# Row tiles in five buffers and earlier accumulator additions in the second output projection of a decoder layer

## The chip, the cores and the metric

The kernel runs on one core of a Trainium2 chip. The metric is device time in microseconds (us) of one execution. An execution was also recorded by the hardware profiler; everything that is said of engines, waits and loads comes from that record. The engines are TensorE (PE in the profile, with its weight loads as PEld), VectorE (DVE), ScalarE (ACT), GpSimd (POOL) and SyncE (SP), which here issues most of the transfers (DMAs) between the chip's main memory and its on-chip memory. Each engine works through its own queue strictly in the order of the program; engines wait for each other by semaphores.

## The reference

The reference is one layer of a decoder trunk, in float32, on 1024 positions of 1024 channels. The part around the change:

```python
mix = (jax.nn.sigmoid(gate_a) * y_a + jax.nn.sigmoid(gate_b) * y_b) @ w_o[l]
h = layer_norm(DN_ALPHA * h + mix, ln1_g[l], ln1_b[l])
ffn = conv_ffn(h, w_ffn_up[l], ffn_dw_w[l], ffn_dw_b[l], w_ffn_down[l])
h = layer_norm(DN_ALPHA * h + ffn, ln2_g[l], ln2_b[l])
```

So the product with `w_o` (the output projection) is added to the scaled residual `h`, normalised over the 1024 channels of each position, and the result is what the up projection of the FFN reads.

## The kernel before

The positions are worked in two halves of 512. The first half's normalised rows have long been stored in main memory (`h1_scr`) when the part of this document begins; the second half's output projection is the function `out_proj_pairs`. All products are made in three matmuls each (lines 175, 176 and 177): weights and data are split into a high and a low part, and the product of the two low parts is left out. ScalarE makes the high part (a cast, L141 for weights) and VectorE the low part (a subtraction, L142).

**Rows.** A row tile `r` holds 128 positions by 1024 channels, 4 KB on each partition. `ffn_blocks` makes eight of them under one tag with three buffers: r0 to r3 (`rows`) are the first half's rows, loaded back from `h1_scr` at L927, and r4 to r7 (`rest`) take the second half's residual `h`, loaded at L875. With three buffers, r3 takes the buffer that r0 leaves, r4 that of r1, and so on.

**The first half's rows** are transposed on TensorE (L935, four 128x128 transposes to a bank of PSUM, two banks a row tile), and split into `h1b1` by ScalarE (L940) and VectorE (L941); a plain copy is kept in `h1raw` (L950).

**The second half** is projected in two pairs of row tiles. For each pair there are four PSUM accumulators (tag `acc`, four banks in all), and eight weight tiles `w_wo` are loaded, split and multiplied. Then VectorE adds each accumulator to its half of a row tile (L894), which frees the bank, and `ln_stats` and `ln_apply` normalise the row tiles (statistics at L220 and L234, the root on ScalarE at L235, then L236, L240 and L243). For each finished row tile `block_sums` runs: it stores the row, transposes it, and forms the sums that a Strassen-like scheme for the up projection needs (tiles `ts0`, `ts1` and `ts2`; the results go to `h1s1` to `h1s3` and `h1b2`). GpSimd does the additions L965 and L971 for the first three tiles, VectorE for the fourth.

**What follows.** `up_first` computes, for the first eight column tiles of the FFN's up projection, two products that need only the first half's `h1b1`, so they can run while the second half is being normalised. Its weights are `w_ue0` to `w_ue6` (tag `w` of a pool with three buffers, so that `w_ue3` takes the buffer that `w_ue0` leaves). For each column tile one PSUM bank collects the product with block `b11` (12 matmuls); ScalarE copies it out (`first0_j`, L1015); then the product with block `b21` (12 more) is added on top in the same bank, and copied out again (`first1_j`). The tiles `first` have two buffers and are stored to main memory by DMAs from ScalarE's queue (L1016).

**Memory.** The on-chip memory is given out from two ends. `ffn_blocks` works in a pool `trans` that grows from the left and ends with the function; the pool `firsts` of `up_first` is opened after that at the right, below the block sums' results. In the built program of the kernel before, `trans` ends at byte 169472 of a partition, the last two tiles in it being the two buffers of `ts2`, and `firsts` begins at byte 175872. Where a later tile covers bytes of a tile of an earlier pool, its first writer waits for the last user of the earlier one.

**What sets the order.** A scheduler places the instructions of ScalarE, VectorE, TensorE, GpSimd and SyncE one by one: among those that are ready by its own reckoning the one with the highest priority goes first, priority falling in the order of the code. `tc.high_priority(offset=n)` moves a block ahead by n; the weights' loads and splits have 4000. The order so found is fixed in the program.

Of the kernel before, what the change touches and what calls it, by code (L numbers as in the profile page):

```python
# [8 lines left out]
F32 = mybir.dt.float32  # L9
F32R = mybir.dt.float32r  # L10
AF = mybir.ActivationFunctionType
ALU = mybir.AluOpType
# [4 lines left out]
P = 128  # L17
D = 1024
T = 1024
HALF = 512  # L20
# [8 lines left out]
ALPHA = 2.0 ** 0.25  # L29
# [25 lines left out]
def kernel(  # L55
# [15 lines left out]
    V, A, G, TE, SY = nc.vector, nc.scalar, nc.gpsimd, nc.tensor, nc.sync  # L71
# [14 lines left out]
    def bank(which):  # L86
        n_ps[0] += 1
        pl, tag = (pacc, "acc") if which else (psm, "sm")
        return pl.tile([P, 512], F32, tag=tag, name=f"{tag}{n_ps[0]}")
# [46 lines left out]
    def weights(src, name, pl=None, eng=None, bufs=None):  # L136
        with tc.high_priority(offset=4000):
            st = wst.tile([P, D], F32, tag="st", name=f"st_{name}")
            SY.dma_start(st, src)
            w = (pl or wsp).tile([P, 2, D], F32R, tag="w", bufs=bufs, name=f"w_{name}")  # L140
            A.copy(w[:, 0, :], st)  # L141
            (eng or V).tensor_tensor(  # L142
                out=w[:, 1, :], in0=st, in1=w[:, 0, :].bitcast(F32), op=ALU.subtract
            )
        return w
# [23 lines left out]
    def big_tile(name):  # L169
        return big.tile([P, 2, KD, HALF], F32R, tag="big", name=name)  # L170

    def mm3(ps, wa, xa, start, stop, more=False):


        TE.matmul(ps, wa(0), xa(0), start=start, stop=False, skip_group_check=more)  # L175
        TE.matmul(ps, wa(0), xa(1), start=False, stop=False, skip_group_check=more)  # L176
        return TE.matmul(ps, wa(1), xa(0), start=False, stop=stop, skip_group_check=more)  # L177
# [36 lines left out]
    def row(pl, start, n, name, tag=None):  # L214
        r = pl.tile([P, n], F32, tag=tag or name, name=name)
        SY.dma_start(r, prow[start : start + n].partition_broadcast(P))
        return r
# [4 lines left out]
    def ln_stats(pl, tiles, name, sts=None):  # L222

        n = len(tiles)
        mv = pl.tile([P, n, 2], F32, tag="ln_mv", bufs=2, name=f"mv_{name}")
        rs = pl.tile([P, n], F32, tag="ln_rs", bufs=2, name=f"rs_{name}")
        for i, t in enumerate(tiles):
            if sts:
                st = sts[i]
            else:  # L230
                st = pl.tile([P, 2, 6], F32, tag="ln_st", bufs=2, name=f"st_{name}{i}")
                for q in range(2):
                    ln_part(pl, t, st, q)
            V.bn_aggr(out=mv[:, i, :], in_=st)  # L234
        A.activation(out=rs, in_=mv[:, :, 1], func=AF.Sqrt, bias=eps)  # L235
        V.reciprocal(out=rs, in_=rs)  # L236
        return mv, rs

    def ln_apply(t, mv, rs, i, g, b, op=ALU.subtract):
        V.scalar_tensor_tensor(  # L240
            out=t, in0=t, scalar=mv[:, i, 0:1], in1=g, op0=op, op1=ALU.mult
        )
        V.scalar_tensor_tensor(  # L243
            out=t, in0=t, scalar=rs[:, i : i + 1], in1=b, op0=ALU.mult, op1=ALU.add
        )
# [626 lines left out]
    def out_proj_pairs(pl, rs, mixT, g, b, done):  # L872

        for t in range(4):
            SY.dma_start(rs[t], h_scr[1][t * P : (t + 1) * P, :])  # L875
        for pair in range(2):
            ts = (2 * pair, 2 * pair + 1)
            pss = {(t, q): bank(1) for t in ts for q in range(2)}
            for kp in range(4):
                for q in range(2):  # L880
                    w = weights(wo[q, kp], f"wo1_{pair}_{q}_{kp}")
                    for t in ts:
                        for k in range(2):
                            mm3(
                                pss[t, q],
                                lambda i: mixT[:, i, 2 * kp + k, t * P : (t + 1) * P],
                                lambda i: w[:, i, k * HALF : (k + 1) * HALF],
                                kp == 0 and k == 0,
                                kp == 3 and k == 1,
                            )  # L890
            for t in ts:
                for q in range(2):
                    r = rs[t][:, q * HALF : (q + 1) * HALF]
                    V.scalar_tensor_tensor(  # L894
                        out=r, in0=r, scalar=ALPHA, in1=pss[t, q], op0=ALU.mult, op1=ALU.add
                    )
            for t in ts:
                mv, rstd = ln_stats(pl, rs[t : t + 1], f"o1_{t}")
                ln_apply(rs[t], mv, rstd, 0, g, b)
                done(t)  # L900
# [20 lines left out]
    def ffn_blocks(tp, qp, mixT):  # L921


        g, b = row(tp, RW_1G, D, "ln1_g"), row(tp, RW_1B, D, "ln1_b")
        rows = [tp.tile([P, D], F32, tag="row", bufs=3, name=f"r{t}") for t in range(4)]
        for t in range(4):
            SY.dma_start(rows[t], h1_scr[t * P : (t + 1) * P, :])  # L927

        def by_channels(r):
            pv = []  # L930
            for q in range(2):
                pt = bank(0)
                for i in range(4):
                    c = (4 * q + i) * P
                    TE.transpose(pt[:, i * P : (i + 1) * P], r[:, c : c + P], ident)  # L935
                pv.append(pt.rearrange("p (k t) -> p k t", k=4))
            return pv

        def parts(dst, src):
            A.copy(dst(0), src)  # L940
            V.tensor_tensor(out=dst(1), in0=src, in1=dst(0).bitcast(F32), op=ALU.subtract)  # L941

        b1 = big_tile("h1b1")
        raw = tp.tile([P, KD, HALF], F32, name="h1raw")
        for t in range(4):
            ts = slice(t * P, (t + 1) * P)
            for q, pv in enumerate(by_channels(rows[t])):
                ks = slice(4 * q, 4 * q + 4)
                parts(lambda i: b1[:, i, ks, ts], pv)
                A.copy(raw[:, ks, ts], pv)  # L950
        sums = [qp.tile([P, 2, 4, HALF], F32R, name=f"h1s{i}") for i in (1, 2, 3)]
        rest = [tp.tile([P, D], F32, tag="row", bufs=3, name=f"r{4 + t}") for t in range(4)]
        b2, kept = [], []

        def block_sums(t):
            SY.dma_start(h1_scr[HALF + t * P : HALF + (t + 1) * P, :], rest[t])
            e = V if t == 3 else G
            ts = slice(t * P, (t + 1) * P)
            b12, b22 = by_channels(rest[t])
            t0, t1, t2 = (  # L960
                tp.tile([P, 4, P], F32, tag=f"ts{i}", bufs=n, name=f"ts{i}_{t}")
                for i, n in ((0, 2), (1, 1), (2, 2))
            )
            A.copy(t0, b12)
            e.tensor_tensor(out=t1, in0=raw[:, 0:4, ts], in1=t0, op=ALU.subtract)  # L965
            V.tensor_tensor(out=t0, in0=t0, in1=b22, op=ALU.subtract)
            parts(lambda i: sums[0][:, i, :, ts], b22)
            V.tensor_tensor(out=t2, in0=t0, in1=raw[:, 0:4, ts], op=ALU.subtract)
            parts(lambda i: sums[2][:, i, :, ts], t2)
            parts(lambda i: sums[1][:, i, :, ts], t1)  # L970
            e.tensor_tensor(out=t2, in0=raw[:, 4:8, ts], in1=t2, op=ALU.add)  # L971
            kept.append((ts, t0, t2))
            if t >= 2:
                if not b2:
                    b2.append(big_tile("h1b2"))
                for ks, t3, t4 in kept:
                    parts(lambda i: b2[0][:, i, 0:4, ks], t3)
                    parts(lambda i: b2[0][:, i, 4:8, ks], t4)
                kept.clear()

        out_proj_pairs(tp, rest, mixT, g, b, block_sums)
        return {
            "b11": lambda i: b1[:, i, 0:4, :],
            "b21": lambda i: b1[:, i, 4:8, :],
            "b22": lambda i: sums[0][:, i],
            "t1": lambda i: sums[1][:, i],
            "t2": lambda i: sums[2][:, i],
            "t3": lambda i: b2[0][:, i, 0:4, :],
            "t4": lambda i: b2[0][:, i, 4:8, :],
        }  # L990
# [338 lines left out]
    with pool("rows0") as pl:  # L1329
        rs = [pl.tile([P, D], F32, name=f"r0_{t}") for t in range(4)]  # L1330
# [9 lines left out]
    with pool("trans") as tp:  # L1340
        bl = ffn_blocks(tp, qp, mixT)
# [126 lines left out]
```

## Time and profile before

| | |
|---|---|
| time, 3 runs | 1935.33 us median (1933.6 to 1936.34) |
| the profiled execution | 1934.78 us, its span 1933.1 us |
| TensorE busy | 1917.5 us (99% of the span) |
| VectorE busy | 1636.4 us (85%) |
| ScalarE busy | 1102.3 us (57%) |
| the second output projection, TensorE | 1241.59 us (first matmul with `w_wo`) to 1291.94 us (first with `w_ue`) |
| the products with `h1b1` and the block sums beside them | 1291.94 us to 1335.50 us (first matmul with `h1s`) |

The span is what lies between the first and the last instruction; the profiled execution's time is 1.68 us longer. Times in the profile's rows are us from the start of the span. In a timeline a row is one instruction or several equal ones in a row: its start, the time to its end, engine, line, operation, what it writes and reads, how often, and in brackets the idle time of its engine before it with what ended it. Matmuls overlap: each of 128x512 takes 0.39 us from start to end, but the next one starts 0.23 us after it. Buffer numbers are left out, so `r` stands for r0 to r7, `first` for both buffers.

### The profile page before, as it was taken

The numbers are of one execution on the slowest core, as the hardware profiler recorded it, in microseconds if no ns is written. First come the engines' busy times: TensorE is split into PE (matmuls) and PEld (weight loads), VectorE is DVE, ScalarE is ACT, GpSimd is POOL, SyncE is SP. The second block draws the span as 40 slices with busy tenths as digits, with TensorE's granted clock in tenths as the row PEclk, the third lists the DMA queues.
The fourth block names the chain that finished last, engine by engine and source line by source line (L and its number), as shares of the span: only waits on it lengthen the run. The fifth ranks groups of instructions, "written<-read, shape, count | busy, mean of one in ns | idle before, by whom it ended". The sixth has DMA issues, their size and how long they took to land.

```text
span 1933.1 us, 24959 instructions
## 1 busy us (share of the span) xinstructions
PE 1917.5 (99%) x9138; PEld 1572.3 (81%) x9138; DVE 1636.4 (85%) x2216; ACT 1102.3 (57%) x1842; POOL 136.1 (7%) x184
## 2 busy tenths in 40 slices
PE   8999999999999999999999999999999999999998
PEld 7888888888888887888888888878888888888886
DVE  7699999998566879999999967588998887888868
ACT  6787877464353378767755446365655445453532
POOL 0100000000400010000000040001000000021000
PEclk9999999999999999999999999999999999999999
DMA  6424343524546543433353444566443322368572
GB/s 214 144 99 148 109 132 115 174 104 148 174 137 215 204 131 106 143 120 120 126 169 109 136 169 139 180 243 243 160 156 109 114 104 94 111 238 274 179 260 98
DMA packets 103869, 297.16 MB, mean 154 GB/s; under 512 B 12353, under 2 KB 12513, under 8 KB 103746
## 3 DMA queue, kind: packets, MB, share of 16 engines
q1 hardware_dynamic: 87696, 244.16, 37.2%
q0 software_dynamic: 13744, 47.21, 7.6%
q10 hardware_dynamic: 2306, 4.20, 0.6%
q8 instruction: 71, 1.16, 0.2%
q14 instruction: 52, 0.43, 0.1%
HBM read 245.69 MB, written 49.82 MB: 153 GB/s over the span
## 4 chain that ended last, share of the span: by engine, by line
PE 96%; DVE 1%; ACT 1%; DMA 1%; issue 0%; POOL 0%; DVEq 0%; ACTq 0%; POOLq 0%
PE acc L177 26%; PE acc L175 26%; PE acc L176 26%; PE sm L176 4%; PE sm L177 4%; PE sm L175 4%; PE sm L660 2%; PE sm L606 1%; PE sm L656 1%; PE sm L622 1%; PE acc L345 1%; DMA r<-h_scr 0%; PE sm L626 0%; DMA m<-cum_scr 0%; PE sm L935 0%
## 5 line engine op out<-in xcount | busy, mean ns | idle before, releaser
L546 DVE SCALAR_TENSOR_TENSOR c<-v,pc,c 128x512 f32<-128x512 f32 x480 | 341.4, 743 | 5.7 <-ACT c L535 4.8
L176 PE MATMUL acc<-hT,w_c 128*128 128x512 f32 x368 | 147.8, 402 | 0.0
L175 PE MATMUL acc<-hT,w_c 128*128 128x512 f32 x368 | 145.2, 394 | 0.0
L177 PE MATMUL acc<-hT,w_c 128*128 128x512 f32 x368 | 144.9, 394 | 0.0
L1094 DVE SCALAR_TENSOR_TENSOR fo<-u,pc,fo 128x1024 f32<-128x1024 f32 x88 | 111.0, 1285 | 0.0
L635 ACT ACTIVATE m<-m,cums 128x128 f32<-128x128 f32 x256 | 79.5, 402 | 52.8 <-DMA m<-cum_scr 42.6
L501 DVE SCALAR_TENSOR_TENSOR xbc<-u,pc,xbc 128x512 f32<-128x512 f32 x144 | 104.6, 743 | 0.1
L177 PE MATMUL acc<-h1s,w_s 128*128 128x512 f32 x264 | 102.8, 390 | 0.5 <-DVE w_s L918 0.5
L175 PE MATMUL acc<-h1s,w_s 128*128 128x512 f32 x264 | 102.8, 389 | 0.0
L176 PE MATMUL acc<-h1s,w_s 128*128 128x512 f32 x264 | 102.7, 389 | 0.0
L175 PE MATMUL acc<-hT,w_z 128*128 128x512 f32 x256 | 102.0, 399 | 0.0
L176 PE MATMUL acc<-hT,w_z 128*128 128x512 f32 x256 | 101.8, 398 | 0.0
L177 PE MATMUL acc<-hT,w_z 128*128 128x512 f32 x256 | 101.7, 397 | 0.0
L1241 ACT CAST w_dn<-dr 128x1024 fp32r<-128x1024 f32 (+1 forms) x72 | 60.3, 847 | 61.4 <-DVE dr L1164 28.1
L177 PEld LDWEIGHTS acc<-hT,w_c 128*128 128x128 f32 x368 | 69.2, 188 | 16.6 <-issue 3.0
L176 PEld LDWEIGHTS acc<-hT,w_c 128*128 128x128 f32 x368 | 69.2, 188 | 16.2 <-issue 2.6
L175 PEld LDWEIGHTS acc<-hT,w_c 128*128 128x128 f32 x368 | 69.1, 188 | 15.1 <-issue 1.1
L1242 DVE TENSOR_TENSOR w_dn<-dr,w_dn 128x1024 fp32r<-128x1024 f32 (+1 forms) x72 | 69.6, 972 | 12.7 <-ACT w_dn L1241 12.4
L142 DVE TENSOR_TENSOR w_c<-st_c,w_c 128x1024 fp32r<-128x1024 f32 x46 | 56.0, 1218 | 16.5 <-ACT w_c L141 16.5
L175 PE MATMUL sm<-h1b,w_s 128*128 128x512 f32 x176 | 68.5, 389 | 0.0
L176 PE MATMUL sm<-h1b,w_s 128*128 128x512 f32 x176 | 68.5, 389 | 0.0
L177 PE MATMUL sm<-h1b,w_s 128*128 128x512 f32 x176 | 68.5, 389 | 0.0
(400 smaller groups left out, 5564.1 us busy)
## 6 DMA issues: line engine op xcount, KB each, us to landing
st_c<-wcol SPq DMA_DIRECT2D x46, 512.0 KB, 3.5
st_z<-wz SPq DMA_DIRECT2D x32, 512.0 KB, 3.4
m<-cum_scr POOLq DMA_DIRECT2D x32, 512.0 KB, 4.5
st_wo<-wo SPq DMA_DIRECT2D x24, 512.0 KB, 4.1
ra<-wup SPq DMA_DIRECT2D x22, 512.0 KB, 3.6
rb<-wup SPq DMA_DIRECT2D x22, 512.0 KB, 3.4
t_scr<-fo POOLq DMA_DIRECT2D x22, 512.0 KB, 3.3
dr<-t_scr SPq DMA_DIRECT2D x44, 256.0 KB, 3.5
```

Of the source, the lines that this page charges most:

```text
L142: (eng or V).tensor_tensor(out=w[:, 1, :], in0=st, in1=w[:, 0, :].bitcast(F32), op=ALU.subtract)
L175: TE.matmul(ps, wa(0), xa(0), start=start, stop=False, skip_group_check=more)
L176: TE.matmul(ps, wa(0), xa(1), start=False, stop=False, skip_group_check=more)
L177: return TE.matmul(ps, wa(1), xa(0), start=False, stop=stop, skip_group_check=more)
L345: TE.matmul(ps, w, hT[:, b, k, ts], start=(a, b) == (0, 0) and k == 0, stop=(a, b) == (1 if i else 0, 0 if i else 1) and k == KD - 1,)
L501: V.scalar_tensor_tensor(out=o, in0=u[:, k : k + HALF], scalar=pc[:, wc + k : wc + k + 1], in1=o, op0=ALU.mult, op1=ALU.add,)
L546: V.scalar_tensor_tensor(out=accs[i], in0=v[:, k : k + HALF], scalar=pc[:, wc + k : wc + k + 1], in1=accs[i], op0=ALU.mult, op1=ALU.add,)
L635: A.activation(out=m[:, h, :], in_=m[:, h, :], func=AF.Relu, scale=-1.0, bias=cums[:, c, k : k + 1],)
L660: masked = TE.matmul(py[h % 2 * HP : (h % 2 + 1) * HP, h // 2 * P : (h // 2 + 1) * P], xs[:, h * HP : (h + 1) * HP], m[:, h, :], start=Tru ...
L1094: V.scalar_tensor_tensor(out=o, in0=u[:, k : k + T], scalar=pc[:, wc + k : wc + k + 1], in1=o, op0=ALU.mult, op1=ALU.add,)
L1241: A.copy(w[0][:, cs], src)
L1242: V.tensor_tensor(out=w[1][:, cs], in0=src, in1=w[0][:, cs].bitcast(F32), op=ALU.subtract)
```

## The change

Both allocations of row tiles (`rows` and `rest`) now have five buffers instead of three, so r5 is the first that has to wait for an earlier one (r0), and the pool `trans` is 8 KB larger on each partition. The additions of the accumulators in `out_proj_pairs` stand in a block with priority offset 1500, for both pairs. Nothing that is computed changes.

```diff
@@ out_proj_pairs
-            for t in ts:
-                for q in range(2):
-                    r = rs[t][:, q * HALF : (q + 1) * HALF]
-                    V.scalar_tensor_tensor(
-                        out=r, in0=r, scalar=ALPHA, in1=pss[t, q], op0=ALU.mult, op1=ALU.add
-                    )
+            with tc.high_priority(offset=1500):
+                for t in ts:
+                    for q in range(2):
+                        r = rs[t][:, q * HALF : (q + 1) * HALF]
+                        V.scalar_tensor_tensor(
+                            out=r, in0=r, scalar=ALPHA, in1=pss[t, q], op0=ALU.mult, op1=ALU.add
+                        )
@@ ffn_blocks
-        rows = [tp.tile([P, D], F32, tag="row", bufs=3, name=f"r{t}") for t in range(4)]
+        rows = [tp.tile([P, D], F32, tag="row", bufs=5, name=f"r{t}") for t in range(4)]
...
-        rest = [tp.tile([P, D], F32, tag="row", bufs=3, name=f"r{4 + t}") for t in range(4)]
+        rest = [tp.tile([P, D], F32, tag="row", bufs=5, name=f"r{4 + t}") for t in range(4)]
```

Lines behind L891 move by one in the changed kernel (L894 becomes L895, L935 L936, L940 and L941 L941 and L942, L1015 L1016). The same number of instructions stands on each engine; the scheduler has placed them otherwise in three places that matter. In the rows below the number behind a name's first part tells the tile (`r6` is the seventh row tile, `w_ue0` the weights of the first column tile, `first0_0` its first product), and the brackets name the engines or DMA rings whose semaphore the instruction waits for.

The loads on SP's queue during the projection, in the kernel before from the load of r2 on:

```order
L927 DMA r2_10439<-h1_scr_122 128x1024 [waits DMASW1_49]
L139 DMA st_wo1_0_1_3_10645<-wo 128x1024 [waits DMAHW7_49,DVE_49]
L139 DMA st_wo1_1_0_0_10740<-wo 128x1024 [waits DMAHW0_49,DVE_49]
L927 DMA r3_10440<-h1_scr_122 128x1024 [waits DMAHW3_49,DMAHW1_49,PE_49]
L139 DMA st_wo1_1_1_0_10757<-wo 128x1024 [waits DMAHW5_49,DMAHW2_49,DVE_49]
L875 DMA r4_10514<-h_scr1_121 128x1024 [waits DMAHW4_49,PE_49]
L139 DMA st_wo1_1_0_1_10774<-wo 128x1024 [waits DMAHW7_49,DVE_49]
L139 DMA st_wo1_1_1_1_10791<-wo 128x1024 [waits DMAHW0_49,DVE_49]
L875 DMA r5_10515<-h_scr1_121 128x1024 [waits DMAHW6_49,PE_49]
```

and in the changed one:

```order
L928 DMA r2_10439<-h1_scr_122 128x1024
L928 DMA r3_10440<-h1_scr_122 128x1024 [waits DMAHW7_49]
L875 DMA r4_10514<-h_scr1_121 128x1024 [waits DMAHW0_49,DMASW1_49]
L139 DMA st_wo1_0_1_3_10645<-wo 128x1024 [waits DMAHW1_49,DVE_49]
L139 DMA st_wo1_1_0_0_10740<-wo 128x1024 [waits DMAHW2_49,DVE_49]
L875 DMA r5_10515<-h_scr1_121 128x1024 [waits DMAHW3_49,PE_49]
L139 DMA st_wo1_1_1_0_10757<-wo 128x1024 [waits DMAHW5_49,DMAHW4_49,DVE_49]
L875 DMA r6_10516<-h_scr1_121 128x1024 [waits PE_49]
L139 DMA st_wo1_1_0_1_10774<-wo 128x1024 [waits DMAHW6_49,DMAHW1_49,DVE_49]
L875 DMA r7_10517<-h_scr1_121 128x1024 [waits DMAHW7_49,PE_49]
```

Here r3 and r4 have moved ahead of two weight tiles and no longer wait for TensorE, and r5, r6 and r7 have each moved ahead of weights too.

TensorE's queue behind the projection, changed kernel, one row for each change of bank or weights (the rows of an equal kind between them are left out):

```order
L175 MATMUL acc417_10985<-h1b1_10445,w_ue0_10982 128x512 [waits DVE_49,Activation_49]
...
L175 MATMUL acc418_11021<-h1b1_10445,w_ue1_11018 128x512 [waits DVE_49,Activation_49]
...
L175 MATMUL acc419_11057<-h1b1_10445,w_ue2_11054 128x512 [waits DVE_49,Activation_49]
...
L936 MATMUL sm413_10891<-ident_75,r6_10516 128x128 [waits DVE_49,PE_49]
...
L936 MATMUL sm415_10939<-ident_75,r7_10517 128x128 [waits DVE_49]
...
L175 MATMUL acc417_10985<-h1b1_10445,w_ue0_10982 128x512 [waits Activation_49]
L176 MATMUL acc417_10985<-h1b1_10445,w_ue0_10982 128x512
```

In the kernel before, the second product with `w_ue0` (`acc417`, waiting for ScalarE) stands third, behind 24 matmuls with `w_ue0` and `w_ue1`, and 86 matmuls stand ahead of the transposes of r6; now 36 do, and the second product with `w_ue0` comes behind the transposes of r6 and r7.

ScalarE's queue, kernel before, from the copy of the first product on:

```order
L1015 COPY first0_0_10998<-acc417_10985 128x512 [waits PE_49]
L940 CAST h1s1_10511<-sm408_10717 128x4x128 [waits DVE_49]
L940 CAST h1b2_10915<-ts0_1_10722 128x4x128
L1016 DMA first_scr0_123<-first0_0_10998 128x512 [waits Activation_49]
L940 CAST h1b2_10915<-ts2_0_10689 128x4x128 [waits Pool_49]
L141 CAST w_ue3_11090<-st_ue3_11088 128x1024 [waits DMAHW2_49,PE_49]
```

and in the changed one, up to that copy:

```order
L965 COPY ts0_2_10901<-sm413_10891 128x512 [waits PE_49,Activation_49]
L965 COPY ts0_3_10949<-sm415_10939 128x512 [waits PE_49,Activation_49]
L941 CAST h1s2_10512<-ts1_2_10902 128x4x128 [waits Pool_49]
...
L941 CAST h1b2_10915<-ts2_2_10903 128x4x128 [waits Pool_49]
L941 CAST h1s3_10513<-ts2_3_10951 128x4x128 [waits DVE_49]
L941 CAST h1b2_10915<-ts2_3_10951 128x4x128 [waits DVE_49]
L1016 COPY first0_0_10998<-acc417_10985 128x512 [waits DVE_49]
L1017 DMA first_scr0_123<-first0_0_10998 128x512 [waits Activation_49]
L141 CAST w_ue3_11090<-st_ue3_11088 128x1024 [waits DMAHW2_49,PE_49]
```

The copy of the first product has moved behind all of ScalarE's work for the block sums, and waits for VectorE instead of TensorE. In the built program `trans` now ends at byte 177664, the second buffer of `ts2` lying from 175616 on, and `firsts` still begins at 175872: the two cover 1792 common bytes. The VectorE instruction that the copy waits for is the last one that reads `ts2`, the subtraction `h1b2<-ts2_3` (L942). On VectorE's queue the split of `w_ue3` (L142), which stood ahead of the normalisation of r6, has moved behind that subtraction.

## The prediction

> **What bounds the kernel now.** I read the page first, busy times and the chain that ended last.
>
> ```profile
> PE 1917.5 (99%) x9138; PEld 1572.3 (81%) x9138; DVE 1636.4 (85%) x2216; ACT 1102.3 (57%) x1842; POOL 136.1 (7%) x184
> PE 96%; DVE 1%; ACT 1%; DMA 1%; issue 0%; POOL 0%; DVEq 0%; ACTq 0%; POOLq 0%
> ```
>
> TensorE is the bound almost everywhere: it idles 15.6 us of the span of 1933.1 us. So a change elsewhere pays only what TensorE waits for, and whatever makes TensorE wait anew is paid in full, since there is no idle time in which to catch up. Next the view of waits for TensorE, its rows on this part of the program:
>
> ```profile
> PE acc L175 <- DVE r L894: 1.0, 1, 1.0
> PE acc L177 <- DVE w_s L918: 0.5, 1, 0.5
> PE acc L177 <- DVE w_ue L142: 0.3, 1, 0.3
> ```
>
> The first is the wait that the change is about. TensorE's timeline around it, then the chain, then the SP queue's issue:
>
> ```profile
> 1270.07 0.39 PE L175 MATMUL acc<-w_wo,mixT 128*128 128x512 f32 x1
> 1271.46 0.50 PE L175 MATMUL acc<-w_wo,mixT 128*128 128x512 f32 x1 [1.00 <-DVE r L894]
> 1271.80 0.40 PE L176 MATMUL acc<-w_wo,mixT 128*128 128x512 f32 x1
> ...
> 1263.92 6.78 DMA r<-h_scr
> 1270.72 0.70 DVE r L894
> ...
> 1263.92 0.33 SPq L875 DMA_DIRECT2D r<-h_scr  x1
> ```
>
> The load of r5 is issued at 1263.92, lands 6.78 us later, VectorE adds an accumulator to it, and only then is the bank free for the second pair. Between the two matmul starts lie 1.39 us instead of 0.23, and the next start is 0.11 us late as well (0.34 instead of 0.23): 1.3 us lost.
>
> **The change part by part.** *What it can gain.* With five buffers r5 needs r0's buffer, free as soon as r0's transposes are done, and its load stands three places earlier. That takes the 1.3 us away; at the least nothing (another wait in its place). The row loads now pass weights on SP's queue:
>
> ```profile
> 9.50:11.00 1.50, 1.50 (x11) 1.50 (x11) 1.50 (x3) 0.00 (x0) 0.00 (x0) 1.00 1.03 421
> 1258.34 1.08 ACT L141 CAST w_wo<-st_wo 128x1024 fp32r<-128x1024 f32 x1
> 1262.39 0.62 PE L175 MATMUL acc<-w_wo,mixT 128*128 128x512 f32 x2
> ```
>
> At 421 GB/s, the most that this trace moves in such a stretch, 512 KB take 1.25 us; two row tiles ahead of `w_wo` make its cast 2.5 us later at most, 1260.8 to 1261.9 instead of 1258.3 to 1259.4. TensorE wants that tile at 1262.4, and now does 16 transposes (1.75 us) before it: it stays hidden, with 2.2 us to spare. I price it at 0; without that cover each late weight tile would cost at most the 1.25 us by which a row moves it.
>
> *The first new wait: r6 is not ready.* Behind the projection TensorE now has 36 matmuls before it must transpose r6, where it had 86.
>
> ```profile
> 1291.94 0.39 PE L175 MATMUL acc<-h1b,w_ue 128*128 128x512 f32 x1
> 1294.44 0.39 PE L177 MATMUL acc<-h1b,w_ue 128*128 128x512 f32 x1
> ...
> 1312.34 1.03 PE L935 MATMUL sm<-ident,r 128*128 128x128 f32 x8
> 1313.13 0.48 PE L177 MATMUL acc<-h1b,w_ue 128*128 128x512 f32 x1
> ```
>
> Twelve starts, 2.50 us for eleven steps: 0.227 us a matmul, so 36 take 8.2 us. Beginning 1.3 us earlier, at 1290.6, TensorE comes to the transposes at 1298.8. VectorE's path to r6:
>
> ```profile
> 1290.38 0.69 DVE L966 TENSOR_TENSOR ts<-ts,sm 128x512 f32<-128x512 f32 x1 [1.19 <-POOL ts L965]
> 1304.74 1.18 DVE L142 TENSOR_TENSOR w_ue<-st_ue,w_ue 128x1024 fp32r<-128x1024 f32 x1
> 1305.83 0.69 DVE L941 TENSOR_TENSOR h1s<-ts,h1s 128x512 fp32r<-128x512 f32 x1
> 1307.78 2.25 DVE L240 SCALAR_TENSOR_TENSOR r<-r,mv_o,ln_g 128x1024 f32<-128x1024 f32 x1
> 1310.02 1.26 DVE L243 SCALAR_TENSOR_TENSOR r<-r,rs_o,ln_b 128x1024 f32<-128x1024 f32 x1
> ```
>
> From 1290.38 to the end of L243 at 1311.28 VectorE works without a gap, 20.9 us. The earlier additions change little in it: all four still stand among the same subtractions. The split of `w_ue3` goes out (1304.74 to 1305.83, 1.1 us) and one subtraction comes in (0.6 us): 20.4 us. If it starts 1.3 us earlier too, r6 is ready at 1309.5, 10.7 us after TensorE came. It can be less: its start hung on a cast that waited for a late load,
>
> ```profile
> 1286.88 1.05 ACT L141 CAST w_ue<-st_ue 128x1024 fp32r<-128x1024 f32 x1 [2.32 <-DMA st_ue<-wup]
> 1287.84 1.06 ACT L964 COPY ts<-sm 128x512 f32<-128x512 f32 x2
> ```
>
> of which 1.8 us would come off, and the 2.25 us of L240 might be 1.26: 7.9 us. It can be 12.0 if VectorE does not start earlier. I take 9.3, midway between 7.9 and 10.7, as the late load and the slow L240 may or may not come again. The split of `w_ue2`, wanted by TensorE before, falls inside this wait.
>
> *The second new wait: the copy of the first product.* Behind the transposes TensorE's next product adds into `acc417`, which ScalarE must first copy out. That copy now stands behind all casts of the block sums, and its tile lies on bytes of `ts2`, so VectorE's last subtraction has to be done. In the kernel before it ran at once:
>
> ```profile
> 1296.06 0.58 ACT L1015 COPY first<-acc 128x512 f32<-128x512 f32 x1
> 1314.45 0.60 ACT L964 COPY ts<-sm 128x512 f32<-128x512 f32 x1
> 1315.19 1.29 POOL L965 TENSOR_TENSOR ts<-h1raw,ts 128x512 f32<-128x512 f32 x1 [6.25 <-ACT ts L964]
> 1316.52 0.69 DVE L966 TENSOR_TENSOR ts<-ts,sm 128x512 f32<-128x512 f32 x1 [1.17 <-POOL ts L965]
> 1321.49 2.00 DVE L142 TENSOR_TENSOR w_ue<-st_ue,w_ue 128x1024 fp32r<-128x1024 f32 x1
> 1323.42 0.68 DVE L968 TENSOR_TENSOR ts<-ts,h1raw 128x512 f32<-128x512 f32 x1
> 1328.52 0.69 DVE L941 TENSOR_TENSOR h1b<-ts,h1b 128x512 fp32r<-128x512 f32 x1 [0.69 <-ACT h1b L940]
> ```
>
> From r6 ready: four transposes (0.9 us at the low clock of the next paragraph), ScalarE's copy 0.6, GpSimd 1.3, with handovers 3.2 us in all; then VectorE's 16 operations, 1316.52 to 1329.21, 12.7 us, less the 1.9 us of the split at 1321.49 that has moved behind them: 10.8 us; then the copy with its handovers, 0.7 us. Together 14.7 us, in which TensorE has 16 transposes to do, 1.75 us at full clock (8 cost 0.88 us by the rows at 1312.34: two of the next starts are late too). Lost: 12.9 us; between 11.3 (no gaps, full clock) and 14.2 us (a second slow GpSimd operation). What is queued behind the copy on ScalarE is the cast of `w_ue3`, and behind that all copies of `up_first`, for which TensorE waits in turn.
>
> *The clock.* Both waits leave TensorE idle long. After the last matmul of the program the granted clock reads:
>
> ```profile
> 1924.49 0.39 PE L177 MATMUL acc<-last 128*128 128x512 f32 x1
> ...
> 1927.00:1928.50 1.50, 0.00 (x0) 0.00 (x0) 1.46 (x4) 0.16 (x1) 0.00 (x0) 1.00 0.00 0
> 1928.50:1929.00 0.50, 0.00 (x0) 0.00 (x0) 0.50 (x1) 0.00 (x0) 0.00 (x0) 0.86 0.00 0
> 1929.00:1930.00 1.00, 0.00 (x0) 0.00 (x0) 0.80 (x2) 0.00 (x0) 0.00 (x0) 0.50 0.01 2
> ...
> 6.45 4.67 PE L332 MATMUL acc<-ones 128*128 128x128 f32 x22
> 11.83 0.83 PE L332 MATMUL acc<-ones 128*128 128x128 f32 x6
> ```
>
> It falls to half some 4 us after the last matmul. At the program's start equal matmuls come 0.21 us apart for 4.67 us and 0.11 us apart afterwards. So the second restart runs at half for about 4.6 us: 2.3 us lost (0 to 4).
>
> The Trainium skill, "TensorE: Matmul & The Clock Gate", section "What's actually happening", puts the fall behind one idle window of about 3.4 us and the recovery behind a busy one as long; the rows agree in kind with 4 us and 4.7 us. By its window the restart would cost an estimated 1.7 us instead of 2.3, and the sum would be 0.6 us lower.
>
> *The refill.* In the kernel before, the cast of `w_ue3` into the buffer that `w_ue0` leaves lies beside 12 other matmuls; now nothing stands between. TensorE waits for the cast (1.05 us as at 1286.88, 0.2 handover), and then for two copies of 0.5 us behind it less the two matmuls that fit in: 1.8 us; at the least 1.3. At the most 5, if the stores of `first` are slow, as the tile view of `first` shows that they can be:
>
> ```profile
> DMA to landing us min/median/max: 2.0/2.2/6.9
> ```
>
> *What falls away:* the waits of 0.3 and 0.5 us quoted at the top, the first covered, the second perhaps: −0.4 us (0 to −0.8).
>
> **The sum** against the profiled execution's 1934.78 us (span 1933.1 and 1.7 around it): −1.3 + 9.3 + 12.9 + 2.3 + 1.8 − 0.4 = +24.6, 1959.4 us. The runs' median, 1935.33, lies 0.55 us above the profiled execution, a difference well inside what follows. I predict 1959 us.
>
> **The rivals.** *The buffers do what their name says: not slower.* The row tiles are there in time, the wait of 1.3 us goes, and nothing comes after: 1934.78 − 1.3 = 1933.5 us, within 0.2% (3.9 us, about what a measurement of this kernel tells from no change). The place is the transposes of r6: it decides if VectorE's path to r6 ends within the 8.2 us of TensorE's 36 matmuls plus the 1.5 us by which it starts ahead. The path is 20.4 us long and gapless, so VectorE would have to do it in half the time. Against it also stands the second wait, which no load can shorten. 4%. The Trainium skill, "Perfetto Trace Analysis", section "Optimization Strategy", would point this way: it says that repeated gaps can come from too few buffers. The one gap of 1.0 us here fits that, the memory for the buffers is what it does not price.
>
> *Only the first wait is paid.* If the copy of the first product ran when TensorE had it (as at 1296.06), TensorE would lose −1.3 + 9.3, about 0.9 for 8 transposes at half clock and 1 for the restart behind them: +9.9, 1945 us. For it: only the second buffer of `ts2` is covered, by 1792 bytes. Against: that buffer is the fourth row tile's, the last to be finished, and the copy stands behind those casts in ScalarE's order anyway. 5%.
>
> *The refill is starved.* Three weight loads (`rb`, 512 KB each) now leave SP's queue just when the copies' stores start, since they too wait for the block sums' memory. If every store of the first column tiles then takes 6.9 us instead of 2.2, the two buffers of `first` turn over that much later: some 4.7 us more for the first pair and the same again for the second at the most, 1964 to 1969 us. For it: the 6.9 us row. Against: 1.5 MB at 421 GB/s are gone in 3.7 us, and TensorE needs 2.7 us a product at full clock meanwhile. 12%.
>
> **How the numbers follow.** Both waits, with the terms as summed: 77%; 2% for what I have not seen. Its own range, not all bounds at once, is 1952 to 1965 us. Reaching towards the starved refill above and some way to the lone first wait below gives 1950 to 1966 us. All but the first rival are slower than before by more than 0.2%; a gain of 3.9 us is more than the waits quoted here hold, and gets what is left. Slower 94%, within 0.2% 4%, faster 2%.
>
> **What would show it.** TensorE's waits should have two new rows: transposes L936 behind VectorE's r L243, 8 to 12 us, and acc L175 behind ScalarE's first L1016, 11 to 14 us; the row of L894 should be gone. r5's load should be issued near 1257. The granted clock should fall below 1.00 in both gaps, and matmuls behind the second start 0.45 us apart at first. ScalarE's copy of `first` should begin right behind VectorE's last L942 `h1b<-ts`. The products with `h1s` should start some 24 us later than 1335.5, and everything behind them take as long as before. The prediction is wrong if the transposes of r6 run without a long wait, if ScalarE copies `first0_0` before the block sums end, or if the time behind 1335.5 changes by itself.

## The result, and the profile after

| | before | after |
|---|---|---|
| time, 4 runs each | 1934.57 us median (1933.6 to 1936.34) | 1961.55 us median (1959.87 to 1962.72) |
| ratio after to before | | 1.0142, 95% interval 1.013 to 1.0153 |
| the profiled execution | 1934.78 us, span 1933.1 | 1959.87 us, span 1958.2 |
| first matmul with `w_wo` to first with `w_ue` | 1241.59 to 1291.94: 50.35 us | 1241.88 to 1291.19: 49.31 us |
| first with `w_ue` to first with `h1s` | to 1335.50: 43.56 us | to 1361.66: 70.47 us |
| from there to the end of the span | 597.60 us | 596.54 us |

The change costs 1.42%. In the profiled executions the span grew by 25.1 us. The part between the projection and the products with `h1s` alone grew by 26.9 us; the stretches around it became about 1 us shorter each. The page of the changed kernel, busy times and the shares of the chain that ended last:

```profile
PE 1922.0 (98%) x9138; PEld 1577.1 (81%) x9138; DVE 1635.0 (83%) x2216; ACT 1103.2 (56%) x1842; POOL 133.0 (7%) x184
PE 94%; DVE 3%; DMA 1%; ACT 1%; issue 1%; POOL 0%; DVEq 0%; ACTq 0%; POOLq 0%
```

No engine has more instructions; TensorE's 4.5 us more of busy time are for the most part matmuls at the lower clock. TensorE's share of the chain fell from 96 to 94%, VectorE's rose from 1 to 3%: the chain now runs over VectorE for most of the time from 1288.65 to 1324.00 us. The view of waits for TensorE in this part (total, count, longest, in us):

```profile
PE acc L175 <- ACT first L1016: 12.1, 2, 11.9
PE sm L936 <- DVE r L243: 7.8, 1, 7.8
PE acc L177 <- DVE w_ue L142: 1.7, 1, 1.7
PE acc L175 <- ACT w_ue L141: 1.1, 1, 1.1
```

The row of L894 is gone, and two long ones are new, those that the prediction named. TensorE's timeline shows where they stand:

```profile
1291.19 0.39 PE L175 MATMUL acc<-h1b,w_ue 128*128 128x512 f32 x1
...
1298.97 0.50 PE L177 MATMUL acc<-h1b,w_ue 128*128 128x512 f32 x1 [1.71 <-DVE w_ue L142]
...
1301.14 0.39 PE L177 MATMUL acc<-h1b,w_ue 128*128 128x512 f32 x1
1309.31 3.49 PE L936 MATMUL sm<-ident,r 128*128 128x128 f32 x16 [7.78 <-DVE r L243]
1324.67 0.79 PE L175 MATMUL acc<-h1b,w_ue 128*128 128x512 f32 x1 [11.87 <-ACT first L1016]
...
1329.53 0.43 PE L177 MATMUL acc<-h1b,w_ue 128*128 128x512 f32 x1
1331.09 0.50 PE L175 MATMUL acc<-h1b,w_ue 128*128 128x512 f32 x1 [1.13 <-ACT w_ue L141]
...
1361.66 0.39 PE L175 MATMUL acc<-h1s,w_s 128*128 128x512 f32 x1
```

Between 1291.19 and 1301.14 stand the 36 matmuls; then nothing until r6 is normalised, 16 transposes, and nothing again until the first product has been copied out. What the second wait hangs on, by the timelines of VectorE and ScalarE:

```profile
1323.31 0.69 DVE L942 TENSOR_TENSOR h1b<-ts,h1b 128x512 fp32r<-128x512 f32 x1 [0.68 <-ACT h1b L941]
...
1324.03 0.58 ACT L1016 COPY first<-acc 128x512 f32<-128x512 f32 x1 [0.76 <-DVE h1b L942]
...
1330.00 1.04 ACT L141 CAST w_ue<-st_ue 128x1024 fp32r<-128x1024 f32 x1 [5.38 <-PE acc L177]
```

VectorE's last subtraction of the block sums ends at 1324.00, and ScalarE's copy starts at 1324.03. The load of r5 is on time:

```profile
1257.00 0.33 SPq L875 DMA_DIRECT2D r<-h_scr  x1
```

It is issued 6.9 us earlier than before, as the change means it to be. The two waits behind it cost far more than that can gain.

### The profile page after: what moved, and what is told of

It is laid out like the page before. It is cut to its first block, busy times and chain, and to the rows that moved or that the text cites. A ratio compares the mean times of both kernels' runs of the same rounds, so it can differ in the third digit from the quotient of the medians.

```text
span 1958.2 us, 24954 instructions
## 1 busy us (share of the span) xinstructions
PE 1922.0 (98%) x9138; PEld 1577.1 (81%) x9138; DVE 1635.0 (83%) x2216; ACT 1103.2 (56%) x1842; POOL 133.0 (7%) x184
## 4 chain that ended last, share of the span: by engine, by line
PE 94%; DVE 3%; DMA 1%; ACT 1%; issue 1%; POOL 0%; DVEq 0%; ACTq 0%; POOLq 0%
PE acc L175 25%; PE acc L176 25%; PE acc L177 25%; PE sm L175 4%; PE sm L177 4%; PE sm L176 4%; PE sm L660 2%; PE sm L656 1%; PE sm L606 1%; PE sm L622 1%; PE acc L345 1%; DMA st_wo<-wo 1%; PE sm L626 0%; DVE h1s L942 0%; DVE h1b L942 0%
## 5 line engine op out<-in xcount | busy, mean ns | idle before, releaser
L175 PE MATMUL acc<-h1b,w_ue 128*128 128x512 f32 x168 | 66.8, 398 | 13.2 <-ACT first L1016 12.1
```

## The experiments

**What the two edits do to the program.** In the built programs, with the priority block alone (three buffers) every engine's queue holds the same instructions in the same order with the same waits as in the kernel before. With five buffers and no priority block the program is the changed kernel's, again instruction for instruction. So the offset of 1500 moves nothing here: all the scheduler's new order comes from the buffers. One run measures this.

### The priority block alone

```diff
-            for t in ts:
+            with tc.high_priority(offset=1500):
+                for t in ts:
...
         rows = [tp.tile([P, D], F32, tag="row", bufs=3, name=f"r{t}") for t in range(4)]
```

> The priority block alone, row tiles in three buffers as before. Theory (all of the loss comes from the two more row buffers and the bytes they take): the block moves no instruction on any engine, so the time is that of the kernel before, 1934.6 us within 0.2% (3.9 us), with its 1.0 us wait of TensorE behind VectorE's r L895. Rival (the additions that go first push VectorE's subtractions of the block sums back, and these carry part of the loss): 1937 to 1947 us, and a wait at the transposes L936 behind r L243.

Measured: 1934.27 us median of 10 runs against 1934.23, ratio 1.0001 (0.9992 to 1.0011). As the theory had it. TensorE's wait for the late row tile is there, at 0.6 us in this execution:

```profile
PE acc L175 <- DVE r L895: 0.6, 1, 0.6
```

Since the program is that of the kernel before, this execution also tells how far two executions of one program differ: 50.48 us against 50.35 in the projection, 42.96 against 43.56 from there to the products with `h1s`, 598.37 against 597.60 behind.

### 32 bytes of overlap, without any change to the rows

Two kernels: both are the kernel before with an unused tile ahead of the `ts` tiles, and a memset of one element a partition. The diff is that of the first; the second has 1608 for 1600, 32 bytes more.

```diff
+        pad = tp.tile([P, 1600], F32, name="pad")
+        V.memset(pad[:, 0:1], 0.0)
         sums = [qp.tile([P, 2, 4, HALF], F32R, name=f"h1s{i}") for i in (1, 2, 3)]
```

> The kernel before with an unused tile of 6400 bytes ahead of the ts tiles in the pool trans, which then ends at 175872, exactly where firsts begins: no byte shared. One more VectorE memset of one element a partition. Theory (overlap) and every rival that needs more row buffers: as before, 1934.6 us within 0.2%.

> The same with 6432 bytes: trans ends 32 bytes above the beginning of firsts. Row tiles in three buffers, no priority block, all row loads as before. Theory (any shared byte makes the scheduler place the copy of first0_0 behind all block sums and the transposes behind 36 matmuls): both waits in full, 7 to 8 us at L935 and some 12 us at the copy, and the 1.0 us wait behind r L894 on top: 1962 us (1960 to 1964). Rival (the loss comes from the row loads): 1934.6 us.

Measured: with 6400 bytes, where `trans` ends exactly at `firsts`, 1933.81 us, ratio 0.9999 (0.999 to 1.0009). With 6432 bytes 1961.93 us, ratio 1.014 (1.0125 to 1.0155). TensorE's waits in the second, in the same part of the program:

```profile
PE acc L175 <- ACT first L1017: 13.2, 3, 11.7
PE sm L935 <- DVE r L243: 7.1, 1, 7.1
PE acc L177 <- DVE w_ue L142: 1.7, 1, 1.7
PE acc L175 <- ACT w_ue L141: 1.1, 1, 1.1
```

The whole loss is there with three row buffers, the old order of additions and the old row loads. Neither the loads that pass weights on SP's queue nor the additions have a part in it. It is a step, not a slope: 32 bytes cost 28 us. The wait of 1.0 us behind r L894, which the expectation put on top, is in neither run's view, though both have three buffers: the late load does not cost that much in every execution.

### Four row buffers, which fit

```diff
-        rows = [tp.tile([P, D], F32, tag="row", bufs=5, name=f"r{t}") for t in range(4)]
+        rows = [tp.tile([P, D], F32, tag="row", bufs=4, name=f"r{t}") for t in range(4)]
...
-        rest = [tp.tile([P, D], F32, tag="row", bufs=5, name=f"r{4 + t}") for t in range(4)]
+        rest = [tp.tile([P, D], F32, tag="row", bufs=4, name=f"r{4 + t}") for t in range(4)]
```

> As the change, with four row buffers instead of five: the pool trans ends at byte 173568, 2304 bytes below firsts at 175872, so nothing is covered. Theory (overlap of the two pools): no wait at the transposes of r6, none at the copy of first above 1 us; r5 takes r1's buffer and is loaded one buffer earlier, so the wait of 1.0 us behind r L895 goes; 1933.3 us (1932.8 to 1935.5). Rival (more row buffers let row loads pass the weights' loads, and that costs): half of the loss or more remains with one buffer of the two, 1945 to 1950 us.

Measured: 1935.65 us median of 10 runs, ratio 1.0003 (0.9994 to 1.0013). The loss is gone with the overlap; the gain of 1.3 us does not show either. In the profiled execution TensorE's wait for the row tile has gone and the projection takes 48.90 us instead of 50.35, but the first product with `h1s` now waits for ScalarE (and a later one for 1.13 us, at ScalarE's `s`, L1056, a wait that the kernel before does not have):

```profile
1334.53 1.05 ACT L918 CAST w_s<-ra 128x1024 fp32r<-128x1024 f32 x1
...
1335.63 0.50 PE L175 MATMUL acc<-h1s,w_s 128*128 128x512 f32 x1 [0.33 <-ACT w_s L918]
```

### Five row buffers that fit, and their control

The first half of `h1raw` is read for the last time by the operation that writes `ts2`; so `ts2` can be formed in place there, and its 4 KB are not needed. The pool `trans` then ends at 173568 with five row buffers. The control has the same edit and three row buffers.

```diff
-            t0, t1, t2 = (
+            t0, t1 = (
                 tp.tile([P, 4, P], F32, tag=f"ts{i}", bufs=n, name=f"ts{i}_{t}")
-                for i, n in ((0, 2), (1, 1), (2, 2))
+                for i, n in ((0, 2), (1, 1))
             )
+            t2 = raw[:, 0:4, ts]
```

> Five row buffers and the priority block as in the change, but ts2 is formed in place in the first half of h1raw, which nobody reads afterwards, so its two buffers (4 KB) are not needed and the pool trans ends at 173568, below firsts. Theory (overlap): the same row loads as in the change without its two waits, 1933.3 us (1932.8 to 1935.5): the kernel before less its 1.3 us. Rival (five buffers, their loads or their order cost time by themselves): 1950 us or more, with the 7.8 us wait at L936 still there.

> Three row buffers, no gain from loads; ts2 formed in place in h1raw as in the run with five. It tells what forming ts2 in place does by itself. Theory: nothing, 1934.6 us within 0.2%, with the wait of 1.0 us behind r L895; if it differs, that difference is to be taken off the run with five buffers. Rival (in-place sums wait for GpSimd or for the casts): 1936 to 1940 us, with a new wait of TensorE at the products with h1s.

Measured: five buffers 1937.41 us median of 10 runs, ratio 1.0016 (1.0006 to 1.0025); the control 1936.14 us, ratio 1.0009 (0.9999 to 1.0018). Five buffers do not cost the 27 us, so the rival falls. But the gain did not come: the theory's 1933.3 was missed by 4 us, of which 1.9 us stand in the control too (1936.14 against 1934.23), whose interval just takes in no difference. The wait at the products with `h1s` that the control's rival expects is not in the control's trace. In the profiled execution with five buffers TensorE still waits at the row tiles, and again at the products with `h1s`:

```profile
PE acc L175 <- DVE r L895: 0.7, 1, 0.7
...
1337.88 1.04 ACT L918 CAST w_s<-ra 128x1024 fp32r<-128x1024 f32 x1 [0.98 <-DMA s<-first_scr]
...
1338.98 0.50 PE L175 MATMUL acc<-h1s,w_s 128*128 128x512 f32 x1 [1.48 <-ACT w_s L918]
```

The first row is not the late load of r5, which is issued at 1259.64 here. By the chain, VectorE's addition stands behind a split of `w_wo` whose load took 11.02 us, from 1255.21 on; the projection takes 50.25 us, about as long as before. In the kernel before, ScalarE's cast of that weight tile (1334.39) came just early enough for the matmul at 1335.50. So with four buffers the 1.3 us are gained in the projection and followed by the next waits, at that cast and at `s`; with five buffers they are not gained in this execution. Whether the 1.3 us between the medians of the two kernels (1937.41 and 1936.14) are more than scatter, these runs do not tell.

### Other bytes covered

Five buffers and the overlap of 1792 bytes are kept, but the tiles of `trans` are allocated in another order, `ts` and `h1raw` low, then the row buffers, with r3's on top; the small tiles of the statistics lie lowest. r3's last transposes end by 1264.4 us in this run.

```diff
+        tss = [[tp.tile([P, 4, P], F32, tag=f"ts{i}", bufs=n, name=f"ts{i}_{t}")
+                for i, n in ((0, 2), (1, 1), (2, 2))] for t in range(4)]
+        raw = tp.tile([P, KD, HALF], F32, name="h1raw")
+        for k in (0, 1, 2, 4, 3):
+            for t in range(k, 8, 5):
+                rr[t] = tp.tile([P, D], F32, tag=f"row{k}", bufs=1, name=f"r{t}")
...
-            t0, t1, t2 = (
...
+            t0, t1, t2 = tss[t]
```

> The change with the tiles of trans in another order: the ts tiles and h1raw lie low, and the 1792 bytes that firsts shares now belong to the buffer of r3 alone, whose last reader (its transposes) is done near 1270 us. Theory A (the scheduler goes by the pools: while they share any byte it takes the whole of trans as in use): the order of the queues stays as in the change, the copy of first0_0 still stands behind all casts, and only VectorE's last subtraction (0.7 us) no longer holds it: 1960.8 us (1960 to 1962). Theory B, as the prediction put it (the covered tile's last user sets when the copy can run): the copy runs when TensorE has the product, the second wait of 12 us goes and with it its half clock: 1945 us, or 1934 us if the first wait goes too.

Measured: 1958.42 us, ratio 1.0125 (1.011 to 1.0141). That is Theory A, though 1.6 us below its range of 1960 to 1962. In ScalarE's queue the copy still stands behind the last cast, though the only thing it waits for is the load of r3, issued some 75 us earlier:

```
L965 CAST h1b2_10921<-ts2_3_10460 128x4x128 [waits DVE_49]
L1035 COPY first0_0_10998<-acc417_10985 128x512 [waits DMAHW7_49]
```

In the changed kernel the second of these rows waits for VectorE. The timelines of ScalarE and VectorE in this run, and a row of TensorE's waits:

```profile
1322.15 0.62 ACT L965 CAST h1b<-ts 128x512 fp32r<-128x512 f32 x1 [2.51 <-DVE ts L991]
1322.68 0.58 ACT L1035 COPY first<-acc 128x512 f32<-128x512 f32 x1
...
1322.80 0.69 DVE L966 TENSOR_TENSOR h1b<-ts,h1b 128x512 fp32r<-128x512 f32 x1 [0.68 <-ACT h1b L965]
...
PE acc L175 <- ACT first L1035: 11.1, 2, 10.9
```

The copy now runs beside VectorE's last subtraction, not behind it, and the second wait is 10.9 us instead of 11.9. So of that wait about 1 us is the semaphore that comes with the covered tile; the rest is the place in the queue, which the scheduler gave with either buffer on the shared bytes. That it goes by whole pools fits this; no run looks into the scheduler itself. (The profiled execution reaches the products with `h1s` 118.73 us after the first matmul with `w_wo`, against 119.78: 1.05 us. The medians differ by 3.1 us, with intervals that overlap.)

### TensorE kept busy in the second wait

Extra matmuls without a use are put between the transposes of r7 and the second product with `w_ue0`, in a bank that is cleared afterwards. First 70 of 128x128:

```diff
+        if j == 3:
+            for _ in range(70):
+                TE.matmul(ps[:, :P], bl["b11"](0)[:, 0, :P],
+                          bl["b22"](0)[:, 0, 2 * P : 3 * P], start=True, stop=True)
         for q, block in enumerate(("b11", "b21")):
```

> The change, with 70 extra matmuls of 128x128 (h1b1 with r6's part of h1s1, into the bank that w_ue3's product clears afterwards): 65 of them stand in TensorE's queue between the transposes of r7 and the second product with w_ue0, 5 behind it beside the wait for w_ue3's cast. They fill most of the second wait with work whose result nobody reads. Theory (the restart runs at half clock for about 5 us and that costs 2.7 us): granted clock 1.00 when the copy is done, the 12 matmuls of the restart in 2.7 us instead of 5.4, 1959.0 us (1958.3 to 1959.8). Rival (the restart is bound by ScalarE's cast of w_ue3 and the copies behind it, so the clock does not matter): 1961.5 us within 0.7 us.

Measured: 1961.08 us, ratio 1.0137 (1.012 to 1.0154). It tells nothing on the price of the clock, since the clock was not kept up. Its windows (PE, PEld, DVE, ACT, POOL busy, granted clock, DMA share, GB/s):

```profile
1313.00:1314.00 1.00, 0.71 (x4) 0.31 (x2) 0.69 (x2) 1.00 (x3) 0.24 (x1) 0.60 0.26 102
1317.00:1318.00 1.00, 1.00 (x8) 1.00 (x7) 1.00 (x3) 0.62 (x1) 0.16 (x1) 0.60 0.00 0
1320.00:1321.00 1.00, 1.00 (x7) 1.00 (x6) 1.00 (x3) 0.62 (x1) 0.00 (x0) 0.50 0.00 0
1330.00:1331.00 1.00, 1.00 (x4) 0.77 (x4) 0.00 (x0) 0.00 (x0) 0.00 (x0) 0.57 0.08 29
```

The clock rose with the transposes at 1313.80, fell at 1317.20 with the extra matmuls already running, and stayed at half for 13.7 us in which TensorE counts as fully busy. So a second kernel has 50 matmuls of 128x384 in the same place.

> As the run with 70 matmuls of 128x128, whose clock fell to half in spite of them (PE busy for 11.6 of 12.5 us, granted clock 0.50 from 1317.2 to 1330.9 us). Here 50 matmuls of 128x384 (h1b1 with the parts of r4 to r6 of h1s1) stand in the same place: 0.17 us each at full clock by the rate of the 128x512 ones, 8.5 us together, less time on weights for each column. Theory (the clock follows the columns that stream, not the share of time in which TensorE is called busy; and half clock at the restart costs 2.7 us): granted clock 1.00 at the restart, its 12 matmuls in 2.7 us instead of 5.1, 1959.1 us (1958.3 to 1960.0). Rival 1 (any extra matmul of this kind leaves the clock at half): the 50 take 16 us, the restart is late by some 6 us, 1967 us. Rival 2 (clock full, but the refill behind the cast of w_ue3 takes as long anyway): 1961.5 us within 0.7 us.

Measured: 1960.61 us, ratio 1.0132 (1.0115 to 1.0149). The clock was now full at the restart. The time lies between those of the theory (1959.1) and of rival 2 (1961.5), and the interval, some 3 us either way, takes in both; the trace has to tell them apart, and it shows rival 2. TensorE's timeline, ScalarE's, and three windows:

```profile
1313.88 10.59 PE L1009 MATMUL acc<-h1s,h1b 128*128 128x384 f32 x50 [0.93 <-ACT h1s L941]
1324.70 0.50 PE L175 MATMUL acc<-h1b,w_ue 128*128 128x512 f32 x1 [0.23 <-ACT first L1025]
1328.85 0.50 PE L175 MATMUL acc<-h1b,w_ue 128*128 128x512 f32 x1 [1.13 <-ACT w_ue L141]
1331.32 0.80 PE L175 MATMUL acc<-h1b,w_ue 128*128 128x512 f32 x1 [1.74 <-ACT first L1025]
...
1327.75 1.04 ACT L141 CAST w_ue<-st_ue 128x1024 fp32r<-128x1024 f32 x1 [3.11 <-PE acc L177]
1330.69 0.59 ACT L1025 COPY first<-acc 128x512 f32<-128x512 f32 x1 [1.40 <-DMA first_scr<-first]
...
1317.00:1318.00 1.00, 1.00 (x6) 1.00 (x5) 1.00 (x2) 0.43 (x1) 0.92 (x1) 0.78 0.00 0
1331.00:1332.00 1.00, 0.68 (x2) 0.58 (x3) 0.00 (x0) 0.27 (x1) 0.00 (x0) 0.55 0.21 43
1334.00:1335.00 1.00, 1.00 (x5) 0.76 (x4) 0.00 (x0) 0.00 (x0) 0.00 (x0) 0.75 0.97 391
```

The restart's 12 matmuls now take so little that ScalarE's cast of `w_ue3` starts 3.05 us after the restart (1324.70 to 1327.75) instead of 5.33 (1324.67 to 1330.00): 2.3 us, the size that the prediction gave to the clock. It was not kept. The third copy of `first` needs the first one's buffer, whose store, issued at 1324.67, lands only when the copy starts at 1330.69, some 6 us later; TensorE waits 1.74 us for it, and in that gap, idle for most of 1327.6 to 1331.3, the clock falls once more, from 1331.1 to 1334.5, which costs some 1.6 us. Together that is more than had been gained.

## Why the prediction was right

The forecast, 1959 us with a range of 1950 to 1966, lies 2.6 us below the median of 1961.55, and its likeliest case, both waits, is what happened. Its terms were summed against the profiled execution; so they are compared with the profiled execution of the change, whose time is the lowest of its four. Against the +24.6 us of the sum stand +25.1 us. That they agree so closely is in part luck: the profiled executions of the kernel before and of the priority block alone, one and the same program, are 1.7 us apart (1934.78 and 1936.50 us), and the terms below 1 us are no surer than that.

| term | predicted | measured | from |
|---|---|---|---|
| late load of r5 gone | −1.3 | −1.0 | projection 50.35 to 49.31 us |
| first wait | +9.3 | +9.5 | 1.71 at `w_ue2` and 7.78 at the transposes |
| second wait | +12.9 | +13.6 | 1309.31 to 1324.67, less 1.75 for 16 transposes at full clock |
| clock at the restart | +2.3 | +2.3 | cast of `w_ue3` behind the restart, 5.33 against 3.05 us |
| refill | +1.8 | +1.4 | 1.13 for the cast and 0.24 for the copy behind it |
| waits that fall away | −0.4 | −1.4 | 0.3 us at `w_ue`, and 1.06 us in the rest of the program |

Measured, the terms add up to 24.4 us; 0.3 us come from the stage ahead (the first matmul with `w_wo` at 1241.88 instead of 1241.59), and 0.4 us I cannot place.

**The first wait.** VectorE's path was to be 20.4 us; it ran from 1288.65, 1.7 us earlier than before, to about 1309.2, 20.5 us. The late cast at its head did come off in part; one slow L240 stayed, the two L240 together take 3.47 us in VectorE's timeline below, where two of the quicker kind (1.26) would take 2.5. That the split of `w_ue2` would fall inside the wait was right in the sum but not in the place: it stopped TensorE for 1.71 us between the matmuls, which then reached the transposes that much later.

```profile
1303.78 3.47 DVE L240 SCALAR_TENSOR_TENSOR r<-r,mv_o,ln_g 128x1024 f32<-128x1024 f32 x2
...
1307.89 2.47 DVE L243 SCALAR_TENSOR_TENSOR r<-r,rs_o,ln_b 128x1024 f32<-128x1024 f32 x2
```

**The second wait** was 0.7 us larger than summed: VectorE's 16 operations took 11.5 us (1312.52 to 1324.00) instead of 10.8. The sum took off 1.9 us for the split at 1321.49 that has moved away, as long as it lasted in the kernel before. Splits of that size elsewhere take 1.2 us; this one ran beside a GpSimd addition (1321.12 to 1322.41). The slow operation did not go with the split. In the changed kernel it is the subtraction that runs beside that addition (1317.08 to 1318.35 in GpSimd's timeline), where others of its size take 0.69:

```profile
1317.45 1.45 DVE L942 TENSOR_TENSOR h1s<-ts,h1s 128x512 fp32r<-128x512 f32 x1
```

The five kernels whose pools overlap all show it there (1.44 to 1.47 us). Why the two slow down together no run here shows. The prediction gave two reasons for the wait, the copy's place in ScalarE's queue and the byte overlap with `ts2`'s second buffer. The runs part them: the place is worth some 11 us, the semaphore on the covered buffer about 1 us (11.9 against 10.9, one execution each). For the rival of the lone first wait (1945 us) this settles the argument: it had counted in its favour that only one buffer of `ts2` is covered. With r3's buffer covered in place of `ts2`'s, or 32 bytes in place of 1792, the copy stands behind all casts just the same, and 36 matmuls ahead of the transposes of r6.

**The clock and the refill** came out near their sizes, but they are not two terms that can be taken away one by one. With the clock full, the refill waited for a store and for another fall of the clock, and gave the 2.3 us back. The starved refill, which the prediction kept as a rival at 1964 to 1969 us, thus lies right behind: the changed kernel escapes it because its slow restart gives the store the time. The longest landing of `first` in the changed kernel is 5.7 us, by the tile view, against a median of 2.5:

```profile
DMA to landing us min/median/max: 2.0/2.5/5.7
```

**The waits that fall away** were the term with the largest miss, 1.0 us. The 0.5 us behind `w_s` L918 has gone, presumably since the weights get ahead in the long waits, and the rest of the program runs 596.54 us instead of 597.60; what else makes up the 1.06 us no row shows. The prediction had named a change there by itself as a sign of being wrong. It is one of 1 us. The other kernels with the overlap show it too (596.46, 596.45 and 596.44 us, but 598.46 in the run with 50 matmuls, which has a wait of 1.6 us of its own there); the six kernels without the overlap took 597.60 to 599.87 us.

**The rival that the buffers do what their name says** gave 1933.5 us. The gap of 1.0 us that spoke for it stands once in this part of the program and does not repeat, and other executions with three buffers show 0.6, 0.2 or none there; it was a weak sign of too few buffers. Even where they fit, with four or with five buffers, the time is not below that of the kernel before. Its condition, that VectorE's path must end within TensorE's matmuls, was the right one: where the pools do not overlap, 86 or 96 matmuls stand ahead of the transposes of r6 and the two waits are gone. The 1.3 us that should then remain as a gain do not show in the time. With four buffers they are followed by waits of 0.33 and 1.13 us for ScalarE, which the prediction did not name; with five they were not gained in the execution profiled. What sets the medians is left open.

## What to carry to other kernels

Before a pool is given more buffers, compare its new end with where the next pool begins: here an overlap of 32 bytes was enough for the scheduler to put work of the next stage behind all of the last, and the price is set by that order, not by the bytes. Read the queues of the engines behind the change (here TensorE's 36 instead of 86 matmuls ahead of the transposes, and ScalarE's copy behind all casts) and price each against the path it now waits for. A term that is paid behind a wait can be right in size and still not be a gain when it is removed: look for what is ready just behind it.

## What the runs showed of the hardware

**The clock changes on a grid.** From windows of 1 us the moment of a change can be worked out, since the clock reads 1.00 or 0.50: in the changed kernel

```profile
1305.00:1306.00 1.00, 0.00 (x0) 0.00 (x0) 1.00 (x2) 0.00 (x0) 1.00 (x1) 0.84 0.00 0
1312.00:1313.00 1.00, 0.80 (x5) 0.56 (x3) 0.48 (x1) 0.80 (x2) 0.48 (x1) 0.74 0.51 205
1315.00:1316.00 1.00, 0.00 (x0) 0.00 (x0) 1.00 (x3) 0.00 (x0) 0.00 (x0) 0.96 0.00 0
1329.00:1330.00 1.00, 0.96 (x3) 0.34 (x2) 0.00 (x0) 0.00 (x1) 0.00 (x0) 0.71 0.55 209
```

it fell at 1305.68, rose at 1312.52, fell at 1315.92 and rose at 1329.58. The steps are 6.84, 3.40 and 13.66 us: 2, 1 and 4 times 3.42. The run with 70 matmuls of 128x128 gives 1313.80, 1317.20 and 1330.86: 1 and 4 times. The run with 50 matmuls of 128x384 gives 1303.78, 1317.44, 1331.10 and 1334.50: 4, 4 and 1 times. So whether the 3.5 us of transposes between the two waits lift the clock depends on how they lie on this grid: they did in the changed kernel, for 3.4 us in which TensorE then had nothing to do, and did not in the run with 50 matmuls, where the grid cuts them in two at about 1310.6. The Trainium skill, "TensorE: Matmul & The Clock Gate", section "What's actually happening", says as much: a window of 3413 ns that runs freely. The traces agree.

**Busy by the profile is not busy for the clock.** 65 matmuls of 128x128 in fp32r kept TensorE at 1.00 busy from 1315 to 1326 us. The clock fell in their midst, at the end of a window of which they had filled some three quarters (1314.64 to 1317.20), and stayed at half until 1330.86, 4.6 us into the 128x512 matmuls behind them. 50 matmuls of 128x384 in the same place lifted it by 1317.44. The Trainium skill, in that section, says that the warm-up is a matter of time and not of the number of matmuls; for the 128x128 ones here, two whole windows (1317.20 to 1324.0) and most of a third were not enough, and the clock rose at the end of the fourth, which the 128x512 ones filled. That the share of time in which columns stream decides would fit (128x128 ones come 0.18 us apart, with the weight loads at 1.00 busy), but no run here shows it.
